# One-half feed-forward blocks beside the RWKV mixer: down projection in plain float32 products, and slots rounded to 64 bytes

## The chip, the cores and the metric

The kernel runs on one core of a Trainium2 chip. The metric is the device time of one execution in microseconds (us). Four compute engines matter here: TensorE (PE in the profile, with its weight loads as PEld), VectorE (DVE), ScalarE (ACT), and SyncE (SP), which issues all the loads.

## The reference, cut to what matters

Two layers work on 256 tokens of width 1024. Each layer is a feed-forward block, a token mixer with a memory attention, and a second feed-forward block, each followed by a layer norm. Layer 0 mixes with RWKV-7, a recurrence over tokens; layer 1 with stick-breaking attention.

```
swiglu(x, w_gate, w_up, w_down) = (silu(x @ w_gate) * (x @ w_up)) @ w_down     # d_ff = 2816

for i in range(2):
    x = layer_norm(ALPHA*x + 0.5*swiglu(x, ffn1[i]), ...)
    proj = x @ w_in[i]
    mix = rwkv7_mix(proj) if i == 0 else stick_breaking_mix(proj)
    x = layer_norm(ALPHA*x + concat(mix, memory_attention(proj)) @ w_out[i], ...)
    x = layer_norm(ALPHA*x + 0.5*swiglu(x, ffn2[i]), ...)
```

All inputs and the output are float32.

## The kernel before

**Tiles.** The 256 tokens are two halves of 128 (hf 0 and 1), the partitions of every tile. A feed-forward block is cut along d_ff into 11 blocks c of 256 columns (`FC`, `NFC`). One block for one half is 8 steps of a gate/up product (contraction over 1024, 512 columns wide: 256 gate and 256 up), the gating on ACT and DVE, a transposition of the 128x256 result by PE, and the down product: 2 steps of contraction times 2 column halves of 512.

**Split products.** A weight piece of 128x1024 is loaded into a `raw` buffer; ACT copies it to a rounded float32r tile `hi`, and DVE subtracts to get the rest, `lo` (`piece`, L636). The activations are split the same way (`split_T`, L675). `mm3` (L664) then makes one product of float32 operands as three float32r matmuls: hi by hi, hi by lo, lo by hi. There are 10 raw buffers and 9 each of hi and lo (`NRAW`, `NHI`, `NLO`). A raw buffer is free again when `lo` has been made; hi and lo are free when the last matmul has read them. A block needs six pieces: four of gate and up, two of down. The vectors of a layer norm sit in two raw buffers, too.

**Stages.** Half 1 runs behind half 0, so that one half's mixer, a long chain of small steps, has feed-forward blocks of the other half beside it. `LAGS` (L47) says how many blocks of a feed-forward are done for each half alone ("solo"); the rest are "shared": their pieces are loaded and split once and used for both halves (`spread`, L1415). For layer 0 the order is: blocks of FFN1 for half 0 (5 solo and 6 shared), norm of half 0, RWKV of half 0 with the 5 solo blocks of half 1 beside it (the first of them, `HEAD`, just ahead of it), norm of half 1, `w_out` and norm of half 0, RWKV of half 1 with solo blocks of FFN2 of half 0 beside it (`alternate`, L1403), `w_out` and norm of half 1, the last two solo blocks of half 0 (`HOLD`, L52), then the solo blocks of half 1 and the shared ones.

**Order.** The program is not written in the order in which it runs. `Plan` records every operation with a guessed duration; `order` (L346) is a list scheduler with priorities, which also hands out buffers, and `improve` (L542) repeats it with the latest start times as priorities, some noise, and a fixed seed. The numbers in `RW` (L50) say how far the blocks advance at each step of the mixer when the program is recorded, so they set the first priorities only. Any change of the recorded operations therefore gives another order everywhere behind it. Within an engine the order is then fixed, and all loads stand in one queue, SP's: a load whose buffer isn't free holds back those behind it. `copy` (L209) may go to ACT or DVE as the scheduler likes.

**Names.** The profile shows the buffers: `raw_*`, `hi_*`, `lo_*`; `xTh` and `xTl`, the split, transposed input of a stage; `h_*`, a block's gated result; `hT_*` and `pT_*` (one tag, `tb`, with two slots), its transposition; `ps_29` and `ps_30`, the gate/up banks; `ps_25` to `ps_28`, the down sums of half 0 (25, 26) and half 1 (27, 28); `ps_2` and `ps_3`, banks of transpositions and of the mixer; `S`, `T`, `Tt`, `Y`, `L`, `Lm`, `Sk`, `lb`, `vn`, `kn`, `bn`: the mixer's own. All recorded operations have the line of the issuing loop, L599.

**Slots.** All tiles of one tag share slots of the largest size asked for (`slot`, L165); the tag `tb` holds up to 4 x 129 floats, 2064 bytes a partition, so its second slot begins 2064 bytes after the first, rounded up to 32 by the allocator.

Of the kernel before, what the change touches and what calls it, by code (L numbers as in the profile page):

```python
# [13 lines left out]
F32 = mybir.dt.float32  # L14
F32R = mybir.dt.float32r
# [6 lines left out]
P = 128  # L22
D = 1024
# [19 lines left out]
NRAW = 10  # L43
NHI = 9
NLO = 9
HEAD = 1
LAGS = ((5, 9), (4, 8))  # L47
FIRST = 2
PRE = (0, 3)
RW = dict(p0=0, p1=2, p2=0, p3=0, p4=0, lb=0, sub=14, rb=0, kq=1, nat=0.5, dy=3, dt=2, c0=1.0, c1=1, c2=1.5, c3=2, t0=12, t1=10)  # L50
SB = dict(z0=3.0, z1=0, ln=2.0, e0=1.0, e1=1.5, o=6.0)
HOLD = (2, 4)  # L52
TAIL = (2, 2)
# [3 lines left out]
SHY = 1000.0  # L57
BOOST = 18.0075
BESIDE = (True, False)


BLK = 16
_LEVELS = [16, 32]

# [66 lines left out]
class Plan:  # L131
# [33 lines left out]
    def slot(self, pool, shape, dtype, tag, name, bufs):  # L165

        handle = bass.PSumTensorHandle if pool.name == "ps" else bass.SBTensorHandle
        tile = handle(name, list(shape), dtype)[:]
        key = pool.name, tag
        self.tag_of[name] = key  # L170
        self.pools[key] = pool
        self.slots[key] = max(bufs, self.slots.get(key, 0))
        self.size[key] = max(int(np.prod(shape[1:])), self.size.get(key, 0))
        return tile

    def region(self, ap):
# [426 lines left out]
def kernel(ctx, tc, const, x, mem, f1g, f1u, f1d, f2g, f2u, f2d, ln_g, ln_b, w_out, w_mem_kv,  # L603
                      rw_in, r_mu, r_w0, r_wup, r_a0, r_aup, r_gup, r_kk, r_ka, r_rk, r_lng, r_lnb, sb_in, out):
    nc = Plan(tc.nc)
# [4 lines left out]
    def nm(s):  # L610
        uid[0] += 1
        return f"{s}_{uid[0]}"

    def new(pool, shape, dtype, tag, name, bufs=1):

        return nc.slot(pool, shape, dtype, tag, nm(name), bufs)
# [19 lines left out]
    def piece(shape, *srcs):  # L636

        n = int(np.prod(shape))
        hi = new(wp, [P, D], F32R, "hi", "hi", NHI)[:, :n]
        lo = new(wp, [P, D], F32R, "lo", "lo", NLO)[:, :n]  # L640
        raw = new(wp, [P, D], F32, "raw", "raw", NRAW)[:, :n]
        v = lambda t: t.rearrange("p (a b) -> p a b", a=shape[0]) if len(shape) == 2 else t
        m = shape[-1] // len(srcs)
        made = [nc.sync.dma_start(v(raw)[..., i * m:(i + 1) * m], src) for i, src in enumerate(srcs)]
        for o in made:
            nc.in_turn("load", o)
        first = nc.scalar.activation(hi, raw, AF.Copy)
        nc.in_turn("hi", first)
        made.append(nc.vector.tensor_sub(lo, raw, hi.bitcast(F32)))
        nc.in_turn("lo", made[-1])  # L650
        nc.lead.update((o.i, first.i) for o in made + [first])
        return v(hi), v(lo)
# [11 lines left out]
    def mm3(o, sh, sl, wh, wl, start, stop):  # L664
        with nc.together():
            nc.tensor.matmul(o, sh, wh, start=start, stop=False)
            nc.tensor.matmul(o, sh, wl, start=False, stop=False)
            nc.tensor.matmul(o, sl, wh, start=False, stop=stop)
# [13 lines left out]
    def to_T(src, dst, j0, n):  # L682

        for g in range(0, n, 4):
            m = min(4, n - g)
            pt = ps("tp")
            with nc.together():
                for i in range(m):
                    nc.tensor.transpose(pt[:, i * P:(i + 1) * P], src[:, (g + i) * P:(g + i + 1) * P], ident)
            split_T(pt, dst, j0 + g, m)  # L690
# [44 lines left out]
    acc = [None] * NHALF  # L735
# [35 lines left out]
            turn_x(hf)  # L771


    def ffn_block(w, c, halves, beside):
        gv, uv, dv = (m.rearrange("(k p) c -> p k c", p=P) for m in w)
        fs = slice(c * FC, (c + 1) * FC)
        gu = [piece((2, 2 * FC), *(v[:, 2 * g:2 * g + 2, fs] for v in (gv, uv))) for g in range(4)]
        dn = [piece((D,), dv[:, 2 * c + q, :]) for q in range(2)]
        state = {}
        for hf in halves:  # L780
            if todo[hf] == 0:
                open_acc(hf)
                todo[hf] = NFC
            state[hf] = todo[hf] == NFC, todo[hf] == 1
            todo[hf] -= 1

        def down(hf, hh, hl):
            first, last = state[hf]
            for f, n in ((0, 0), (1, 0), (0, 1), (1, 1)) if last else ((0, 0), (0, 1), (1, 0), (1, 1)):
                sl = slice(n * 512, (n + 1) * 512)  # L790
                yield mm3(acc[hf][n], hh[:, f], hl[:, f], dn[f][0][:, sl], dn[f][1][:, sl], first and f == 0, last and f == 1)

        def gated(dst, g, u):

            if beside:
                nc.scalar.activation(dst, g, AF.Tanh, scale=0.5)
                nc.vector.scalar_tensor_tensor(dst, dst, 1.0, g, ALU.add, ALU.mult)
                nc.vector.scalar_tensor_tensor(dst, dst, 0.5, u, ALU.mult, ALU.mult)
            else:
                nc.scalar.activation(dst, g, AF.Silu)  # L800
                nc.vector.tensor_tensor(dst, dst, u, ALU.mult)


        o = {hf: ps("gu") for hf in halves}
        for k in range(KT):
            wh, wl = (t[:, k % 2] for t in gu[k // 2])
            for hf in halves:
                mm3(o[hf], xT[hf][0][:, k], xT[hf][1][:, k], wh, wl, k == 0, k == KT - 1)
            yield
        hs = {}  # L810
        for hf in halves:
            hs[hf] = new(tp_, [P, FC], F32, "ta", "h", 2)
            gated(hs[hf], o[hf][:, :FC], o[hf][:, FC:])

        def turn_h():
            res = []
            for hf in halves:
                hT = new(tp_, [P, 2, 2, P], F32R, "tb", "hT", 2)
                to_T(hs[hf], (hT[:, 0], hT[:, 1]), 0, 2)
                res.append(down(hf, hT[:, 0], hT[:, 1]))  # L820
            return res

        return turn_h
# [574 lines left out]
    def run(*gens):  # L1398
        for g in gens:
            for _ in g:  # L1400
                pass

    def alternate(main, fill, steps):  # L1403

        due = 0.0
        n = next(main, None)
        while n is not None:
            due += steps.get(n, 0)
            while due >= 1.0:
                next(fill, None)  # L1410
                due -= 1.0
            n = next(main, None)
        run(fill)
# [4 lines left out]
        seq += [((i + 0.49) / len(shared), c, range(NHALF)) for i, c in enumerate(shared)]  # L1418
        return [(c, h) for _, c, h in sorted(seq, key=lambda t: t[0])]

    def blocks(w, seq, beside=False):
        waiting = []
        for c, halves in seq:
            hidden = yield from ffn_block(w, c, halves, beside)
            yield from chain(*waiting)
            waiting = hidden()
        yield from chain(*waiting)

    def solo(hf, cs):
        return [(c, [hf]) for c in cs]  # L1430
# [5 lines left out]
    for i in range(DEPTH):  # L1436
        mixer, steps = ((rwkv, RW), (stick, SB))[i % 2]
        last = i == DEPTH - 1
        lag1, lag2 = LAGS[i]
        w = f1g[i], f1u[i], f1d[i]  # L1440
        if i == 0:
            seq = spread((0, range(lag1)), range(lag1, NFC))
            run(blocks(w, seq[:2]))
            nc.in_turn("load", nc.sync.dma_start(cst[:, P:], const[:, P:]))
            run(blocks(w, seq[2:4]))
            rwkv_constants()
            gb = ln_g[i, 0], ln_b[i, 0]
            run(blocks(w, seq[4:]))
        else:
            run(blocks(w, solo(0, range(FIRST))))  # L1450
            gb = ln_g[i, 0], ln_b[i, 0]
            run(blocks(w, spread((0, range(FIRST, lag1)), range(lag1, NFC))))
        norm(0, 2.0 * ALPHA, 4.0 * LN_EPS, gb)
        mixed = []
        run(blocks(w, solo(1, range(HEAD)), BESIDE[0]))
        if i == 0:
            run(memory_kv())
        alternate(chain_steps(mixer(0, mixed)), blocks(w, solo(1, range(HEAD, lag1)), True), steps)
        norm(1, 2.0 * ALPHA, 4.0 * LN_EPS, gb)
        gb = ln_g[i, 1], ln_b[i, 1]  # L1460
        w = f2g[i], f2u[i], f2d[i]
        second = chain_steps(mixer(1, mixed))
        for _ in range(PRE[i]):
            next(second)
        run(chain_steps(mixed_out(0, mixed[0], w_out[i])))
        norm(0, ALPHA, LN_EPS, gb)
        alternate(second, blocks(w, solo(0, range(lag2 - HOLD[i])), True), steps)
        run(chain_steps(mixed_out(1, mixed[1], w_out[i])), blocks(w, solo(0, range(lag2 - HOLD[i], lag2)), BESIDE[1]))
        norm(1, ALPHA, LN_EPS, gb)
        gb = ln_g[i, 2], ln_b[i, 2]  # L1470
        run(blocks(w, spread((1, range(TAIL[i], lag2)), range(lag2, NFC))))
        norm(0, 2.0 * ALPHA, 4.0 * LN_EPS, gb, last)
        run(blocks(w, solo(1, range(TAIL[i]))))
        norm(1, 2.0 * ALPHA, 4.0 * LN_EPS, gb, last)
# [25 lines left out]
```

## Time and profile before

| | us |
|---|---|
| median of 3 runs (1101.57 to 1103.51) | 1103.34 |
| span of the profiled execution, first to last instruction | 1099.8 |
| PE busy | 1062.8 (97%) |
| DVE busy | 928.8 (84%) |
| ACT busy | 751.6 (68%) |

The profiled execution's own time is given by its span; the median of the runs lies 3.5 us above that (launch and end). The page cuts the span into 40 slices; a stage has other limits than the whole, so the windows of a stage are read for what bounds it. A matmul's shown duration (some 390 ns for 512 columns) is longer than the distance between two starts (some 230 ns), since they are pipelined: PE's busy share hides short gaps, and distances between starts are what a product costs. The same holds on DVE, less strongly.

### The profile page before, as it was taken

Reading aid. Unit: us, or ns where it says so; the run is one execution under the profiler, and the core shown is the slowest. Engines: PE = TensorE matmul, PEld = TensorE weight load, DVE = VectorE, ACT = ScalarE, POOL = GpSimd, SP = SyncE. Lnnn points to the kernel's source line nnn. Section 1 sums busy time; section 2 is a strip of 40 time slices with the busy share of each in tenths; the row PEclk is TensorE's granted clock in tenths of the full one; section 3 lists DMA queues with packets and bytes.
Section 4 is the critical chain, followed back from the end, with each engine's and each line's share of the span. In section 5 each row is a group of like instructions: output and inputs, shape, how many; then the busy total and the mean of one; then the engine's idle time right before and its main releaser. Section 6 shows DMA issues by size and latency. Waiting matters only on the chain.

```text
span 1099.8 us, 17711 instructions
## 1 busy us (share of the span) xinstructions
PE 1062.8 (97%) x6265; PEld 861.4 (78%) x6265; DVE 928.8 (84%) x1312; ACT 751.6 (68%) x1021; POOL 2.7 (0%) x14
## 2 busy tenths in 40 slices
PE   7999999998799999999999999999999999999996
PEld 6878887876678787778888888888877877888885
DVE  6567677999999999998889965649899989987777
ACT  7466566987369786676668654547898898866652
POOL 0000000000000000000000000000000000000000
PEclk9999999999989999999999999999999999999998
DMA  9499758866679587799989976657987987998781
GB/s 344 149 363 378 262 203 291 295 216 204 190 226 336 179 288 251 256 297 369 323 271 362 352 244 212 206 195 258 392 292 269 349 284 266 376 379 292 264 289 59
DMA packets 212250, 303.30 MB, mean 276 GB/s; under 512 B 13844, under 2 KB 159424, under 8 KB 212162
## 3 DMA queue, kind: packets, MB, share of 16 engines
q1 hardware_dynamic: 212162, 302.18, 80.5%
q8 instruction: 49, 0.80, 0.3%
q14 instruction: 39, 0.32, 0.1%
HBM read 301.08 MB, written 1.05 MB: 275 GB/s over the span
## 4 chain that ended last, share of the span: by engine, by line
PE 79%; DVE 13%; DMA 3%; issue 2%; ACT 2%; SPq 0%; DVEq 0%; ACTq 0%
PE ps_30r L599 25%; PE ps_29r L599 24%; PE ps_26r L599 6%; PE ps_25r L599 6%; PE ps_28r L599 6%; PE ps_27r L599 6%; PE ps_2r L599 3%; PE ps_3r L599 3%; DVE x L599 1%; DMA raw_45r<-in_ffn_w_up_dram 1%; DVE lo_44r L599 1%; DVE lb_498r L599 1%; DMA raw_21r<-in_ffn_w_up_dram 1%; DVE lo_20r L599 1%; DVE lo_17r L599 1%
## 5 line engine op out<-in xcount | busy, mean ns | idle before, releaser
L599 ACT ACTIVATE h_32r<-ps_30r 128x256 f32<-128x256 f32 (+1 forms) x35 | 15.1, 431 | 23.1 <-PE ps_30r L599 23.1
L599 ACT ACTIVATE h_31r<-ps_29r 128x256 f32<-128x256 f32 (+1 forms) x34 | 14.5, 426 | 18.5 <-PE ps_29r L599 18.5
L599 PE MATMUL ps_30r<-hi_22r,xTh 128*128 128x512 f32 x64 | 26.3, 410 | 0.0
L599 PE MATMUL ps_30r<-hi_22r,xTl 128*128 128x512 f32 x64 | 25.0, 391 | 0.0
L599 PE MATMUL ps_30r<-lo_23r,xTh 128*128 128x512 f32 x64 | 25.0, 391 | 0.0
L599 PE MATMUL ps_30r<-hi_10r,xTh 128*128 128x512 f32 (+1 forms) x58 | 23.0, 397 | 0.0
L599 PE MATMUL ps_29r<-hi_16r,xTh 128*128 128x512 f32 x56 | 22.4, 401 | 0.0
L599 PE MATMUL ps_29r<-hi_40r,xTh 128*128 128x512 f32 (+1 forms) x56 | 22.4, 401 | 0.0
L599 PE MATMUL ps_30r<-hi_10r,xTl 128*128 128x512 f32 (+1 forms) x58 | 22.3, 385 | 0.0
L599 PE MATMUL ps_30r<-lo_11r,xTh 128*128 128x512 f32 (+1 forms) x58 | 22.2, 383 | 0.0
L599 PE MATMUL ps_29r<-hi_16r,xTl 128*128 128x512 f32 x56 | 21.9, 391 | 0.0
L599 PE MATMUL ps_29r<-lo_17r,xTh 128*128 128x512 f32 x56 | 21.9, 391 | 0.0
L599 PE MATMUL ps_29r<-hi_40r,xTl 128*128 128x512 f32 (+1 forms) x56 | 21.5, 384 | 0.0
L599 PE MATMUL ps_29r<-lo_41r,xTh 128*128 128x512 f32 (+1 forms) x56 | 21.5, 383 | 0.0
L599 PE MATMUL ps_30r<-hi_13r,xTh 128*128 128x512 f32 x52 | 21.4, 412 | 0.0
L599 PE MATMUL ps_30r<-hi_7r,xTh 128*128 128x512 f32 x52 | 21.2, 408 | 0.0
L599 PE MATMUL ps_30r<-lo_14r,xTh 128*128 128x512 f32 x52 | 20.5, 394 | 0.4 <-DVE lo_14r L599 0.4
L599 PE MATMUL ps_2r<-cst,x 128*128 128x128 f32 x48 | 8.9, 316 | 12.2 <-DVE x L599 6.7
L599 PE MATMUL ps_29r<-lo_44r,xTh 128*128 128x512 f32 x50 | 19.7, 395 | 0.9 <-DVE lo_44r L599 0.8
L599 PE MATMUL ps_30r<-lo_17r,xTh 128*128 128x512 f32 x50 | 19.7, 393 | 0.8 <-DVE lo_17r L599 0.8
L599 PE MATMUL ps_30r<-hi_7r,xTl 128*128 128x512 f32 x52 | 20.4, 392 | 0.0
L599 PE MATMUL ps_30r<-hi_13r,xTl 128*128 128x512 f32 x52 | 20.4, 392 | 0.0
(1923 smaller groups left out, 4044.8 us busy)
## 6 DMA issues: line engine op xcount, KB each, us to landing
raw_45r<-in_ffn_w_down_dram SPq DMA_DIRECT2D x17, 512.0 KB, 4.1
raw_24r<-in_ffn_w_down_dram SPq DMA_DIRECT2D x16, 512.0 KB, 4.6
raw_15r<-in_ffn_w_gate_dram SPq DMA_DIRECT2D x30, 256.0 KB, 4.6
raw_15r<-in_ffn_w_up_dram SPq DMA_DIRECT2D x30, 256.0 KB, 5.6
raw_21r<-in_ffn_w_down_dram SPq DMA_DIRECT2D x15, 512.0 KB, 6.3
raw_39r<-in_ffn_w_gate_dram SPq DMA_DIRECT2D x30, 256.0 KB, 4.8
raw_39r<-in_ffn_w_up_dram SPq DMA_DIRECT2D x30, 256.0 KB, 4.9
raw_42r<-in_ffn_w_down_dram SPq DMA_DIRECT2D x15, 512.0 KB, 5.1
```

What stands on the lines that cost most here:

```text
L599: fn(*[at(x) for x in a], **{n: at(x) for n, x in k.items()})
```

## The change

In blocks that a list `WHOLE` names, the two down pieces are loaded into raw buffers and used as they are: no `hi`, no `lo`. The transposed result is copied once, unsplit, and the down product is one plain float32 matmul in place of three float32r ones. The list is asked for only in the solo blocks beside the RWKV mixer and right ahead of and behind it. It names all five of FFN1 for half 1, and of FFN2 for half 0 all but block 3. A second edit moves one block of layer 0's FFN2 from solo to shared (`LAGS`, 9 to 8), so that seven solo blocks of half 0 are whole: twelve in all, 48 products. Four step numbers in `RW` change, and slot sizes are rounded up to 16 floats.

```diff
-LAGS = ((5, 9), (4, 8))
+LAGS = ((5, 8), (4, 8))
-RW = dict(p0=0, p1=2, ..., rb=0, ..., dy=3, ..., t0=12, t1=10)
+RW = dict(p0=0, p1=0, ..., rb=0.5, ..., dy=4, ..., t0=0, t1=10)
+WHOLE = (((0, 1, 2, 3, 4, 5, 6, 8, 9, 10), (0, 1, 2, 4, 5, 6, 7, 8, 9)), ((), ()))
+LINE = 16
...
-        self.size[key] = max(int(np.prod(shape[1:])), self.size.get(key, 0))
+        self.size[key] = max(-(-int(np.prod(shape[1:])) // LINE) * LINE, self.size.get(key, 0))
...
-        dn = [piece((D,), dv[:, 2 * c + q, :]) for q in range(2)]
+        if whole:
+            dn = [new(wp, [P, D], F32, "raw", "raw", NRAW) for _ in range(2)]
+            for q, t in enumerate(dn):
+                nc.in_turn("load", nc.sync.dma_start(t, dv[:, 2 * c + q, :]))
+        else:
+            dn = [piece((D,), dv[:, 2 * c + q, :]) for q in range(2)]
...
+                if whole:
+                    yield nc.tensor.matmul(acc[hf][n], h[0][:, f], dn[f][:, sl], start=start, stop=stop)
+                else:
+                    yield mm3(acc[hf][n], h[0][:, f], h[1][:, f], dn[f][0][:, sl], dn[f][1][:, sl], start, stop)
...
+                if whole:
+                    hT = new(tp_, [P, 2, P], F32, "tb", "hT", 2)
+                    nc.copy(hT, turned(hs[hf], 0, 2))
+                    res.append(down(hf, hT))
...
-        run(blocks(w, solo(1, range(HEAD)), BESIDE[0]))
+        run(blocks(w, solo(1, range(HEAD)), BESIDE[0], WHOLE[i][0]))
-        alternate(second, blocks(w, solo(0, range(lag2 - HOLD[i])), True), steps)
+        alternate(second, blocks(w, solo(0, range(lag2 - HOLD[i])), True, WHOLE[i][1]), steps)
```

On PE, in the first mixer just behind the scores of the memory attention (`memKT`), a block's down product stood like this before:

```order
L599 MATMUL ps_26r<-memKT,mq_357r 128x256
L599 MATMUL ps_3r<-cst,h_32r 128x128 x2
L599 MATMUL ps_27r<-hi_43r,hT_502r 128x512
L599 MATMUL ps_27r<-lo_44r,hT_502r 128x512
L599 MATMUL ps_27r<-hi_43r,hT_502r 128x512
L599 MATMUL ps_28r<-hi_43r,hT_502r 128x512
```

At the same place the changed program has (`pT_352r` is the slot in which the transposed result lies):

```order
L601 MATMUL ps_26r<-memKT,mq_353r 128x256
L601 MATMUL ps_3r<-cst,h_32r 128x128 x2
L601 MATMUL ps_30r<-hi_19r,xTh 128x512
L601 MATMUL ps_30r<-lo_20r,xTh 128x512
L601 MATMUL ps_30r<-hi_19r,xTl 128x512
L601 MATMUL ps_27r<-raw_39r,pT_352r 128x512
L601 MATMUL ps_28r<-raw_39r,pT_352r 128x512
L601 MATMUL ps_27r<-raw_45r,pT_352r 128x512
L601 MATMUL ps_28r<-raw_45r,pT_352r 128x512
```

Twelve matmuls became four, and three gate/up matmuls stand ahead of them. On SP, at the end of the first mixer, the loads of the norm's vectors and of `w_out` stood in these buffers before:

```order
L599 DMA raw_9r<-in_ln_g_dram 128x1024
L599 DMA raw_12r<-in_ln_b_dram 128x1024
L599 DMA raw_39r<-in_w_out_dram 128x2x512
L599 DMA raw_42r<-in_w_out_dram 128x2x512
L599 DMA raw_18r<-in_w_out_dram 128x2x512
L599 DMA raw_24r<-in_w_out_dram 128x2x512
L599 DMA raw_15r<-in_w_out_dram 128x2x512
L599 DMA raw_21r<-in_w_out_dram 128x2x512
```

In the changed program they stand in these, with the whole down pieces of the last blocks in `raw_15r` and `raw_18r` and others:

```order
L601 DMA raw_21r<-in_ln_g_dram 128x1024
L601 DMA raw_42r<-in_ln_b_dram 128x1024
L601 DMA raw_45r<-in_w_out_dram 128x2x512
L601 DMA raw_9r<-in_w_out_dram 128x2x512
L601 DMA raw_12r<-in_w_out_dram 128x2x512
L601 DMA lb_475r<-in_rwkv_lnx_b_dram 128x768
L601 DMA raw_24r<-in_w_out_dram 128x2x512
L601 DMA raw_45r<-in_w_out_dram 128x2x512
L601 DMA raw_9r<-in_w_out_dram 128x2x512
```

`raw_45r` and `raw_9r` are loaded again by the fourth load behind the last one into them (of those into raw buffers); before, it was the eighth at the soonest, everywhere in the program. On DVE the same twelve blocks lose 24 `lo` subtractions and 12 of the split results, and the block that is now shared loses six more `lo` (540 to 510 in the program).

More of the change, by code (lines that the diff above doesn't have):

```diff
@@ L46 @@
 HEAD = 1
-LAGS = ((5, 9), (4, 8))
+LAGS = ((5, 8), (4, 8))
 FIRST = 2
 PRE = (0, 3)
-RW = dict(p0=0, p1=2, p2=0, p3=0, p4=0, lb=0, sub=14, rb=0, kq=1, nat=0.5, dy=3, dt=2, c0=1.0, c1=1, c2=1.5, c3=2, t0=12, t1=10)
+RW = dict(p0=0, p1=0, p2=0, p3=0, p4=0, lb=0, sub=14, rb=0.5, kq=1, nat=0.5, dy=4, dt=2, c0=1.0, c1=1, c2=1.5, c3=2, t0=0, t1=10)
 SB = dict(z0=3.0, z1=0, ln=2.0, e0=1.0, e1=1.5, o=6.0)
@@ L771, in norm, with ffn_block @@
             turn_x(hf)
-    def ffn_block(w, c, halves, beside):
+    def ffn_block(w, c, halves, beside, whole):
         gv, uv, dv = (m.rearrange("(k p) c -> p k c", p=P) for m in w)
@@ L785, in ffn_block, with down @@
             todo[hf] -= 1
-        def down(hf, hh, hl):
+        def down(hf, *h):
             first, last = state[hf]
@@ L790, in down @@
                 sl = slice(n * 512, (n + 1) * 512)
-                yield mm3(acc[hf][n], hh[:, f], hl[:, f], dn[f][0][:, sl], dn[f][1][:, sl], first and f == 0, last and f == 1)
+                start, stop = first and f == 0, last and f == 1
+                if whole:
+                    yield nc.tensor.matmul(acc[hf][n], h[0][:, f], dn[f][:, sl], start=start, stop=stop)
+                else:
+                    yield mm3(acc[hf][n], h[0][:, f], h[1][:, f], dn[f][0][:, sl], dn[f][1][:, sl], start, stop)
         def gated(dst, g, u):
@@ L817, in turn_h @@
             for hf in halves:
-                hT = new(tp_, [P, 2, 2, P], F32R, "tb", "hT", 2)
-                to_T(hs[hf], (hT[:, 0], hT[:, 1]), 0, 2)
-                res.append(down(hf, hT[:, 0], hT[:, 1]))
+                if whole:
+                    hT = new(tp_, [P, 2, P], F32, "tb", "hT", 2)
+                    nc.copy(hT, turned(hs[hf], 0, 2))
+                    res.append(down(hf, hT))
+                else:
+                    hT = new(tp_, [P, 2, 2, P], F32R, "tb", "hT", 2)
+                    to_T(hs[hf], (hT[:, 0], hT[:, 1]), 0, 2)
+                    res.append(down(hf, hT[:, 0], hT[:, 1]))
             return res
@@ L1419, in spread, with blocks @@
         return [(c, h) for _, c, h in sorted(seq, key=lambda t: t[0])]
-    def blocks(w, seq, beside=False):
+    def blocks(w, seq, beside=False, whole=()):
         waiting = []
         for c, halves in seq:
-            hidden = yield from ffn_block(w, c, halves, beside)
+            hidden = yield from ffn_block(w, c, halves, beside, c in whole)
             yield from chain(*waiting)
@@ L1454 @@
         mixed = []
-        run(blocks(w, solo(1, range(HEAD)), BESIDE[0]))
+        run(blocks(w, solo(1, range(HEAD)), BESIDE[0], WHOLE[i][0]))
         if i == 0:
             run(memory_kv())
-        alternate(chain_steps(mixer(0, mixed)), blocks(w, solo(1, range(HEAD, lag1)), True), steps)
+        alternate(chain_steps(mixer(0, mixed)), blocks(w, solo(1, range(HEAD, lag1)), True, WHOLE[i][0]), steps)
         norm(1, 2.0 * ALPHA, 4.0 * LN_EPS, gb)
@@ L1466 @@
         norm(0, ALPHA, LN_EPS, gb)
-        alternate(second, blocks(w, solo(0, range(lag2 - HOLD[i])), True), steps)
-        run(chain_steps(mixed_out(1, mixed[1], w_out[i])), blocks(w, solo(0, range(lag2 - HOLD[i], lag2)), BESIDE[1]))
+        alternate(second, blocks(w, solo(0, range(lag2 - HOLD[i])), True, WHOLE[i][1]), steps)
+        run(chain_steps(mixed_out(1, mixed[1], w_out[i])), blocks(w, solo(0, range(lag2 - HOLD[i], lag2)), BESIDE[1], WHOLE[i][1]))
         norm(1, ALPHA, LN_EPS, gb)
```

## The prediction

> **What bounds the kernel now.** I read the page first: its busy times, and its slices.
>
> ```profile
> span 1099.8 us, 17711 instructions
> PE 1062.8 (97%) x6265; PEld 861.4 (78%) x6265; DVE 928.8 (84%) x1312; ACT 751.6 (68%) x1021; POOL 2.7 (0%) x14
> PE   7999999998799999999999999999999999999996
> DVE  6567677999999999998889965649899989987777
> PEclk9999999999989999999999999999999999999998
> ```
>
> PE is close to full everywhere, DVE only in slices 8 to 18 and in the second layer's mixers. Slices 10 to 12 (27.5 us each), where PE has gaps and loses clock, lie at the end of the first RWKV mixer. Next I cut windows where DVE closes the statistics of the layer norms (152, 294, 322, 478, 571, 606). Columns: busy us of PE, PEld, DVE, ACT, POOL with counts, granted clock, DMA share, GB/s.
>
> ```profile
> 152.00:228.00 76.00, 75.58 (x425) 61.92 (x424) 69.03 (x116) 60.29 (x87) 0.21 (x1) 1.00 0.82 278
> 228.00:294.00 66.00, 61.49 (x832) 49.26 (x832) 64.36 (x115) 44.25 (x80) 0.20 (x1) 0.97 0.61 204
> 294.00:322.00 28.00, 21.49 (x153) 17.92 (x152) 27.47 (x59) 13.66 (x17) 0.43 (x2) 0.82 0.64 197
> 322.00:400.00 78.00, 76.18 (x573) 60.73 (x572) 77.78 (x142) 64.55 (x105) 0.21 (x1) 1.00 0.80 267
> 400.00:478.00 78.00, 76.50 (x792) 62.08 (x791) 76.23 (x119) 54.79 (x77) 0.00 (x0) 1.00 0.80 263
> 478.00:571.00 93.00, 91.80 (x417) 75.14 (x416) 79.62 (x96) 62.81 (x76) 0.00 (x0) 1.00 0.94 324
> 571.00:606.00 35.00, 35.00 (x163) 28.78 (x162) 34.51 (x49) 27.28 (x33) 0.00 (x0) 1.00 0.98 341
> 606.00:748.00 142.00, 142.00 (x644) 116.66 (x643) 92.36 (x116) 73.21 (x95) 0.00 (x0) 1.00 0.72 237
> ```
>
> From 322 to 478, the second RWKV mixer, DVE works 154.0 of 156 us; from 228 to 294, 64.4 of 66. From 478 on PE is the bound: 142 of 142 us in the plain feed-forward. The chain of waits says the same of the first mixer: in 228 to 303 it runs mostly through DVE, and much of it is `lo` subtractions (start, length, what):
>
> ```profile
> 235.13 1.23 DVE lo_17r L599
> 236.36 1.13 DVE lo_23r L599
> 237.49 1.14 DVE lo_11r L599
> 238.63 1.14 DVE lo_14r L599
> ```
>
> So beside the mixers DVE ends last, outside them PE. The change takes work from DVE beside the mixers and gives work to PE: the question is whether a stretch beside a mixer shortens by more than PE's new work adds elsewhere.
>
> **DVE's relief.** The timeline of DVE gives the price of what goes, as distances between starts (columns: start, duration, instruction).
>
> ```profile
> 263.23 0.40 DVE L599 TENSOR_TENSOR hT_545r<-ps_2r,hT_545r 128x256 fp32r<-128x256 f32 x1
> 263.56 0.40 DVE L599 SCALAR_TENSOR_TENSOR h_32r<-h_32r,ps_30r 128x256 f32<-128x256 f32 x1
> 275.48 1.22 DVE L599 TENSOR_TENSOR lo_44r<-raw_42r,hi_43r 128x1024 fp32r<-128x1024 f32 x1
> 276.61 1.22 DVE L599 TENSOR_TENSOR lo_20r<-raw_18r,hi_19r 128x1024 fp32r<-128x1024 f32 x1
> 277.75 1.22 DVE L599 TENSOR_TENSOR lo_11r<-raw_24r,hi_10r 128x1024 fp32r<-128x1024 f32 x1
> 278.88 0.55 DVE L599 TENSOR_TENSOR Tt_358r<-Tt_358r,ps_3r 128x384 f32<-128x384 f32 x1
> ```
>
> A `lo` costs 1.13 us of DVE's time, a split result (`hT`) 0.33. In passing one sees the recurrence's own step (`Tt`) queued behind three `lo`. Counting `lo` in DVE's order between the norms' statistics: 152 to 294 has 53 instead of 61; 294 to 322 8 for 9; 322 to 478 58 for 75 (eleven by whole pieces, six because one block of FFN2 becomes shared). With the split results that is 8 x 1.13 + 4 x 0.33 = 10.4 us, 1.1 us, and 17 x 1.13 + 9 x 0.33 = 22.2 us (the 9 are seven whole blocks and two gating steps of the moved block). ACT loses as many `hi` copies, which costs and gains nothing: it is busy 44 to 65 us in windows of 66 to 78.
>
> **PE's price.** A plain float32 product of 512 columns by 128 rows does not stand in this trace. The nearest row is one of 384 columns, which the profile shows as two matmuls:
>
> ```profile
> 201.56 0.39 PE L599 MATMUL ps_29r<-hi_16r,xTh 128*128 128x512 f32 x1
> 201.79 0.40 PE L599 MATMUL ps_29r<-lo_17r,xTh 128*128 128x512 f32 x1
> 202.02 0.39 PE L599 MATMUL ps_29r<-hi_16r,xTl 128*128 128x512 f32 x1
> 202.25 0.81 PE L599 MATMUL ps_25r<-gup_108r,zl_340r 128*128 128x384 f32 x2
> 202.90 0.81 PE L599 MATMUL ps_26r<-gup_108r,zl_340r 128*128 128x384 f32 x2
> 203.54 0.60 PE L599 MATMUL ps_3r<-cst,h_32r 128*128 128x128 f32 x4
> ```
>
> The split product is three starts 0.23 apart, 0.69 us. The plain one takes 0.645 for 384 columns, so by columns 0.86 for 512: 0.17 more, 48 times, 8.2 us. Bounds: no longer than the 384-column row itself (0.645: 2.2 us gained), or as long by columns as that row's shown duration of 0.81 (1.08: 18.7 us). I take 0.86, since the two rows at 202.25 and 202.90 follow each other without a gap. The Trainium skill (FP8 and Floating Point Precision, TensorE Precision Notes) counts four passes for a true float32 product. By it the product would cost 4 x 0.23 = 0.92, all 48 of them 11.0 us, and my sum below would end 2.8 us higher; the 384-column row speaks for a little less (0.645, where four passes at 384/512 of 0.23 make 0.69), and I keep the row.
>
> By PE's order, between the transpositions behind each norm, float32r products and whole ones change so: first mixer 360 to 300 and 20 whole (-60 x 0.23 + 20 x 0.86 = +3.4 us); up to half 0's norm 105 to 90 (-3.4); second mixer 447 to 354 and 24 (-0.8); the stretch of 478 to 571 414 to 465 and 4 (+15.2: the shared block is done for both halves there, and the last whole one); all behind it 27 fewer (-6.2: the solo block that half 1 no longer has). Sum +8.2, as it must be.
>
> A new wait: the whole product waits for its load and for one copy of the transposed result, where it waited for two `lo` and a split result. Everything behind it on PE waits with it, first the next gate/up product; as down pieces are loaded a block ahead, I cost this at nothing beyond the rival on raw buffers below.
>
> **Slots.** Products with the two slots of `hT` differ (min/median/max ns):
>
> ```profile
> L599 PE MATMUL ps_26r<-hi_10r,hT_876r x8: 389/390/397, 410.3 to 713.3; 128*128 128x512 f32 x8
> L599 PE MATMUL ps_26r<-hi_22r,hT_903r x6: 392/397/501, 401.7 to 669.5; 128*128 128x512 f32 x6
> ```
>
> `hT_903r` is the second slot, which starts 32 bytes off a multiple of 64; each product with it is 6 ns longer. Half of the 88 half-blocks' 12 down products use it, some 460 after the change: up to 2.8 us, which rounding may take away; at least 0. I take 2. The other tiles are small and on no path.
>
> **Sum.** First mixer: DVE could give 10.4 us, PE needs 3.4 more of it. PE has room there (4.9 us idle from 152 to 294, and clock 0.97), but the recurrence also waits on PE and ACT, so I take two thirds of DVE's relief: -7 (ends -10.4 and +3.4). To half 0's norm: -1.5 (ends -3.4 and 0), since the norm's small steps on DVE stay. Second mixer: DVE's 22.2 us can't all come out, since PE is busy 152.7 of 156 and its work falls by 0.8 only; but its shown busy time hides gaps that a slow chain leaves. I take -9 (ends -22.2 and -0.8). Then +15.2, on a PE that is full: all of it on the path. Behind it -6.2, where PE is full too. Slots -2. Total -10.5: a span of 1089.3 us, and with the 3.5 us by which the median of the runs lies above this span, 1092.8 us.
>
> **The rivals.**
>
> *The chain keeps its length (slower).* If the recurrence is held by its own steps on PE, DVE and ACT rather than by the `lo` between them, the three stretches up to 478 keep their length, and what is left is +15.2 - 6.2 - 2 = +7: 1110.3 us. For it: PE and ACT, not DVE, are on the chain in parts of the first mixer, and clock 0.82 from 294 to 322 shows a chain too thin to keep PE up. Against it: DVE idles 1.6 us from 228 to 294 and 2.0 from 322 to 478. It decides if the three stretches together give less than 7 us.
>
> *DVE sets every microsecond.* All of its relief comes out: -10.4 - 1.1 - 22.2 + 7 = -26.7, 1076.6 us. Against it: PE would then do its work of the second mixer in 134 us instead of 156.
>
> *Raw buffers run short.* A whole piece keeps its raw buffer until its down product, behind the next block's gate/up. In the changed order of SP a raw buffer is loaded again by the fourth load after the last one, at the end of the first mixer and around the last whole blocks; eight to ten before.
>
> ```profile
> raw_45r<-in_ffn_w_down_dram SPq DMA_DIRECT2D x17, 512.0 KB, 4.1
> raw_21r<-in_ffn_w_down_dram SPq DMA_DIRECT2D x15, 512.0 KB, 6.3
> L599 ACT ACTIVATE hi_10r<-raw_21r 128x1024 fp32r<-128x1024 f32 x11 | 11.7, 1065 | 5.9 <-PE ps_27r L599 3.1 <-DMA raw_48r<-in_ffn_w_gate_dram 1.7 <-PE ps_28r L599 0.3
> ```
>
> A buffer's round is 4.1 to 6.3 us to land, 1.1 for `hi`, 1.1 for `lo`: some 8 us, with four buffers a piece each 2.1 us. Beside the mixer a piece is wanted each 2.3 us or so (142 us for 61 `lo`), which still fits. In the stretch from 478 it doesn't: a solo block is 36 x 0.23 = 8.3 us for six pieces, 1.4 us each, and over some nine pieces at depth four PE would wait 9 x 0.7 = 6 us, unless the pieces that are made already cover it: 1099 us.
>
> *It does nothing where it counts.* The scheduler gives back in another place what it gains here: 1103.
>
> **How the numbers follow.** My sum, 0.48 (1084 to 1098); raw buffers 0.18; chain 0.15; all of DVE 0.14; nothing 0.05. A measurement of this kernel tells some 0.2% (2.2 us) from no change. Faster: 0.48 + 0.14 + 0.11 of the raw buffers; same: 0.05, 0.05 of the raw buffers and 0.02 of the chain; slower: the rest, 0.15. The range goes from 1080 to 1107: it leaves out half of the rival at 1077 and somewhat over half of the one at 1110, about 0.16.
>
> **What would show it.** In the new profile: 48 products of `ps_25` to `ps_28` from `raw`, as 96 records some 0.43 us apart; DVE below 95% from 322 to the second norm of half 1; that stretch near 147 us and the first mixer's near 135; 15 us more from there to the next norm; products with the second `hT` slot at 390 ns. The sum is wrong if DVE has new idle time that ends with a landing (raw buffers), or if DVE gets idle time that ends with PE or ACT and the stretches stay (chain); the price of a product is wrong if its records lie closer than 0.4 or further than 0.46 us apart.

## The result, and the profile after

The change is faster by 0.8%: 1094.03 us median of 4 runs (1093.15 to 1096.41) against 1102.78 (1101.57 to 1103.51); ratio 0.9924, 95% interval 0.9912 to 0.9936. The forecast was 1092.8. A second measurement of the same kernel, beside the experiments on slots, gave 1094.16 and a ratio of 0.9922 (0.9910 to 0.9935); its profile has a span of 1092.0 us and is called the second profile below.

The page of the profile after, the same lines as of before, and under them the shares of the chain that ended last:

```profile
span 1094.4 us, 17466 instructions
PE 1067.0 (97%) x6217; PEld 852.9 (78%) x6217; DVE 895.0 (82%) x1269; ACT 719.9 (66%) x991; POOL 2.7 (0%) x14
...
PE   7999999999799999999999999999989999999996
...
DVE  6577676999999998787779965659799989987777
...
PEclk9999999999899999999999999999999999999999
...
PE 90%; DVE 6%; DMA 2%; issue 1%; ACT 1%; SPq 0%; DVEq 0%; ACTq 0%
```

The chain's shares before were:

```profile
PE 79%; DVE 13%; DMA 3%; issue 2%; ACT 2%; SPq 0%; DVEq 0%; ACTq 0%
```

DVE has 34 us less work and PE 4 us more busy time. At the end of the first mixer PE has one slice with gaps where it had two. The chain that ended last is 90% PE and 6% DVE, where it was 79% and 13%. Windows cut at the same events as before (DVE closes a norm's statistics; columns as in the prediction):

```profile
152.00:228.00 76.00, 75.96 (x426) 61.70 (x425) 65.65 (x118) 57.33 (x84) 0.20 (x1) 1.00 0.80 266
228.00:290.00 62.00, 61.68 (x822) 45.04 (x823) 58.28 (x100) 37.91 (x73) 0.39 (x2) 1.00 0.70 241
290.00:317.00 27.00, 21.22 (x143) 17.96 (x138) 25.77 (x54) 13.16 (x17) 0.24 (x2) 0.81 0.66 199
317.00:390.00 73.00, 73.00 (x552) 57.55 (x551) 71.60 (x140) 57.92 (x97) 0.20 (x1) 1.00 0.76 259
390.00:464.00 74.00, 74.00 (x762) 56.40 (x761) 63.86 (x100) 43.62 (x64) 0.00 (x0) 1.00 0.80 261
464.00:572.00 108.00, 108.00 (x476) 85.99 (x475) 83.60 (x100) 66.48 (x84) 0.00 (x0) 1.00 0.88 299
```

In the second mixer DVE works 135.5 of 147 us, where it had 154.0 of 156, and PE's shown gaps are gone there. The chain says it more sharply: before, it runs through DVE for 70 of the 156 us from 322 to 478 (31 of them `lo`), after the change, from 317 to 464, for none: all of it is PE. The bound has moved from DVE to PE. To the tenth, by the starts of the same events:

| stretch | before | after | difference | forecast |
|---|---|---|---|---|
| first RWKV mixer | 141.0 | 137.3 | -3.7 | -7 |
| to half 0's norm | 28.1 | 27.6 | -0.5 | -1.5 |
| second RWKV mixer | 156.4 | 146.5 | -9.9 | -9 |
| to the next norm (one more shared block) | 93.3 | 107.9 | +14.6 | +15.2 |
| all behind it | 528.6 | 522.8 | -5.8 | -6.2 |

The plain product's price, in the timeline of PE (start, shown length, what; the three lines with `raw` are a product each, shown as two records, between a float32r matmul and a transposition):

```profile
466.12 0.39 PE L601 MATMUL ps_30r<-hi_13r,xTl 128*128 128x512 f32 x1
466.34 1.02 PE L601 MATMUL ps_25r<-raw_18r,hT_304r 128*128 128x512 f32 x2
467.20 1.02 PE L601 MATMUL ps_26r<-raw_18r,hT_304r 128*128 128x512 f32 x2
468.06 1.02 PE L601 MATMUL ps_26r<-raw_42r,hT_304r 128*128 128x512 f32 x2
468.92 0.38 PE L601 MATMUL ps_3r<-cst,h_31r 128*128 128x128 f32 x2
```

It is 0.86 us from start to start, as the 384-column row said. Four passes, the count of the Trainium skill (FP8 and Floating Point Precision, TensorE Precision Notes), would be 0.92 us if each took the 0.23 of this trace's float32r matmuls, which is an estimate. For the time, the measured 0.86 decides. It doesn't refute the count: four passes of 0.215 us each would give it, too, and no run here parts the two.

### The profile page after: what moved, and what is told of

Read it like the earlier page. It is cut to its first block, busy times and chain, and to the rows that moved or that the text cites. A ratio compares the mean times of both kernels' runs of the same rounds, so it can differ in the third digit from the quotient of the medians.

```text
span 1094.4 us, 17466 instructions
## 1 busy us (share of the span) xinstructions
PE 1067.0 (97%) x6217; PEld 852.9 (78%) x6217; DVE 895.0 (82%) x1269; ACT 719.9 (66%) x991; POOL 2.7 (0%) x14
## 4 chain that ended last, share of the span: by engine, by line
PE 90%; DVE 6%; DMA 2%; issue 1%; ACT 1%; SPq 0%; DVEq 0%; ACTq 0%
PE ps_30r L601 27%; PE ps_29r L601 27%; PE ps_28r L601 8%; PE ps_27r L601 8%; PE ps_25r L601 7%; PE ps_26r L601 7%; PE ps_2r L601 3%; PE ps_3r L601 3%; DVE x L601 1%; DMA raw_45r<-in_sb_w_in_dram 1%; DMA raw_21r<-in_ffn_w_up_dram 1%; DMA raw_9r<-in_ffn_w_up_dram 1%; DVE lb_475r L601 0%; DVE lo_8r L601 0%; DVE S_110r L601 0%
## 5 line engine op out<-in xcount | busy, mean ns | idle before, releaser
L601 ACT ACTIVATE h_31r<-ps_30r 128x256 f32<-128x256 f32 (+1 forms) x53 | 22.8, 430 | 33.6 <-PE ps_30r L601 33.6
L601 ACT ACTIVATE h_32r<-ps_29r 128x256 f32<-128x256 f32 (+1 forms) x53 | 22.0, 414 | 30.0 <-PE ps_29r L601 29.6
L601 PE MATMUL ps_29r<-hi_37r,xTh 128*128 128x512 f32 x58 | 24.2, 417 | 0.0
L601 PE MATMUL ps_29r<-hi_37r,xTl 128*128 128x512 f32 x58 | 22.7, 392 | 0.0
L601 PE MATMUL ps_29r<-lo_38r,xTh 128*128 128x512 f32 x58 | 22.6, 390 | 0.0
L601 PE MATMUL ps_30r<-hi_16r,xTh 128*128 128x512 f32 x54 | 22.6, 418 | 0.0
L601 PE MATMUL ps_29r<-hi_22r,xTh 128*128 128x512 f32 (+1 forms) x54 | 21.9, 406 | 0.0
L601 PE MATMUL ps_30r<-hi_10r,xTh 128*128 128x512 f32 x54 | 21.9, 405 | 0.0
L601 PE MATMUL ps_30r<-hi_40r,xTh 128*128 128x512 f32 x52 | 21.8, 420 | 0.0
L601 PE MATMUL ps_30r<-hi_16r,xTl 128*128 128x512 f32 x54 | 21.2, 392 | 0.0
```

Of the source, the lines that this page charges most:

```text
L601: fn(*[at(x) for x in a], **{n: at(x) for n, x in k.items()})
```

## The experiments

My theory: the whole pieces' relief of DVE beside the RWKV mixers pays for PE's longer products. Its rivals: the moved block, the new order, the loads.

**Which part of the change it is.** Whole pieces off, the rest of the change on:

```diff
-WHOLE = (((0, 1, 2, 3, 4, 5, 6, 8, 9, 10), (0, 1, 2, 4, 5, 6, 7, 8, 9)), ((), ()))
+WHOLE = (((), ()), ((), ()))
```

> The changed kernel with the list of whole blocks empty: the moved block, the step numbers and the slots stay. Theory (the whole pieces' relief of VectorE beside the RWKV mixers is the gain): moving a block takes 8.3 us of PE work each from the second mixer and from half 1's solo blocks and gives 16.6 us to the stretch behind the mixer, so it is about even; 1098 to 1104 us, VectorE at 97% or more from the first mixer to the end of the second. Rival (the moved block is the gain): 1092 to 1096 us.

Measured: 1107.45 us, ratio 1.0038 (1.0023 to 1.0053): slower than before. The rival is refuted, my range was 3.5 us too low, and "about even" was wrong: the move costs. The windows:

```profile
228.00:295.00 67.00, 60.54 (x805) 47.32 (x805) 66.09 (x110) 44.98 (x79) 0.40 (x2) 1.00 0.71 233
...
322.00:398.00 76.00, 71.77 (x552) 57.42 (x551) 74.89 (x142) 61.49 (x100) 0.21 (x1) 1.00 0.79 263
398.00:475.00 77.00, 74.09 (x779) 58.90 (x778) 73.97 (x113) 51.90 (x73) 0.00 (x0) 1.00 0.73 239
475.00:580.00 105.00, 104.80 (x475) 85.69 (x475) 85.03 (x103) 67.00 (x83) 0.00 (x0) 1.00 0.90 303
```

DVE is again at 96 to 99% beside the mixers, and PE shows 6.5 us idle in the first of these windows and 7.1 in the next two. The moved block shortened the second mixer's stretch by 3.8 us only (152.6), though it took 8.3 us of PE work out, and lengthened the next one by 11.7 (105.0).

The other way round, whole pieces with the old split of solo and shared:

```diff
-LAGS = ((5, 8), (4, 8))
+LAGS = ((5, 9), (4, 8))
```

> The changed kernel with nine solo blocks of FFN2 in layer 0 as before (eight of them whole, 13 whole blocks in all). Theory: most of the gain stays, 1093 to 1098 us. Rival (the moved block is the gain): 1100 us or more.

Measured: 1098.7 us, ratio 0.9956 (0.9942 to 0.9971): the theory's side, a little over its range. So the four kernels are: before 1103.1 (measured beside these two; 1102.2 and 1102.4 beside later experiments), the move without whole pieces 1107.5, whole pieces without the move 1098.7, both 1094.0 to 1094.2. Whole pieces give 4.4 us without the move and 13.3 with it; the move costs 4.4 without them and gives 4.5 with them. The middle two also have the changed step numbers and slots, and whole pieces without the move are 13 blocks, not 12. No run has the step numbers alone; the 13.3 us are free of them, since both kernels have them.

**Is it DVE's work?** The same products on PE, but `hi` and `lo` are made as before and not read (this kernel does work that nothing uses):

```diff
...
+                hi = new(wp, [P, D], F32R, "hi", "hi", NHI)
+                lo = new(wp, [P, D], F32R, "lo", "lo", NLO)
+                first = nc.scalar.activation(hi, t, AF.Copy)
...
+                rest = nc.vector.tensor_sub(lo, t, hi.bitcast(F32))
...
```

> The changed kernel, but hi and lo of the whole pieces are made as well and not read: 24 more subtractions of 1.13 us on VectorE and 24 more copies on ScalarE, all else as in the change, PE's plain float32 products too. Theory (VectorE's queue sets the stretches beside the mixers): both stretches go back to what they took before and PE's price stays, 1104 to 1112 us. Rival (the fewer, longer products of PE or the new order are the gain, and VectorE's work is covered): 1092 to 1098 us.

Measured: 1108.19 us, ratio 1.0041 (1.0027 to 1.0055), 14 us over the change, in the middle of the theory's range. Its windows:

```profile
228.00:293.00 65.00, 61.32 (x776) 43.75 (x776) 63.00 (x106) 44.72 (x79) 0.20 (x1) 1.00 0.65 221
...
322.00:398.00 76.00, 74.12 (x545) 57.71 (x544) 73.73 (x139) 60.52 (x100) 0.21 (x1) 0.98 0.71 239
398.00:474.00 76.00, 74.15 (x760) 55.92 (x759) 72.97 (x110) 50.99 (x73) 0.00 (x0) 1.00 0.76 253
```

DVE is back at 96 to 97%, PE's gaps are back, and the mixers' stretches take 141.1 and 152.7 us: 137.3 and 146.5 in the change, 142.7 and 152.6 without whole pieces. So 10.0 of the 14 us lie beside the mixers; the rest is spread over later stretches and isn't explained here. In the window of the second mixer the chain again runs through DVE, for 28 us, 12 of them `lo`. This kernel also holds more `hi` and `lo` buffers than the change and keeps ACT's copies, and its order differs. ACT's busy time grows as DVE's does (37.9 to 44.7 us in the window from 228, DVE 58.3 to 63.0), but ACT is busy for only 67 to 80% of these windows. What this run shows is that making the split pieces costs the time; that DVE's share in it is the larger is read from the chain and the windows, and the buffers aren't tested apart.

**Is it the order?** Another seed of the search (`SEED` 144 to 145), the same operations:

> The changed kernel with another seed of the order's search (145 for 144): the same operations in another order. It measures how far orders alone differ. Theory: within 4 us of the change's 1094 us, 1090 to 1098. Rival (the gain is a lucky order): 1099 us or more.

Measured: 1096.5 us, ratio 0.9935 (0.9921 to 0.9950). The other order costs 2.3 us and keeps 6.6 us of the gain, so the gain isn't a lucky order of the changed kernel. This is one more order, and the kernel before was measured with one only. Differences of 2 to 3 us between the kernels above, whose orders differ, shouldn't be explained one by one, and the 4.4 and 4.5 of the move are only about twice that.

**Each mixer alone.**

```diff
+WHOLE = (((0, 1, 2, 3, 4), ()), ((), ()))
```

> The changed kernel with whole blocks beside the first RWKV mixer alone (five blocks, 20 products). The kernel without any took 1107.5 us, the change 1094.2. Theory (each mixer's stretch gives its own part: 5.4 us in the first and 6.1 in the second, between these two kernels): 1100 to 1104 us, the first mixer's stretch near 137 us, the second's near 152. Rival (both relieve one shared queue of loads, so that one part alone gives little or nearly all): 1106 or more, or 1097 or less.

Measured: 1102.27 us, ratio 0.9998 (0.9988 to 1.0008). Stretches: 137.2 and 152.0 us, as expected.

```diff
+WHOLE = (((), (0, 1, 2, 4, 5, 6, 7)), ((), ()))
```

> The changed kernel with whole blocks in FFN2 beside the second mixer alone (seven blocks, 28 products). Theory: 1099 to 1104 us, the first mixer's stretch near 142 us, the second's near 147. Rival: as for the first mixer alone.

Measured: 1101.64 us, ratio 0.9994 (0.9985 to 1.0004). Stretches: 142.5 us as expected, and 149.5, which is 2.5 over what was expected. From the 1107.5 without any, the first gives 5.2 us and the second 5.8, together 11.0 of the 13.3 that both give: each stretch pays for itself, and the two nearly add, within what another order moves.

**Raw buffers.** `NRAW` 10 to 12, `NHI` and `NLO` 9 to 8:

> The changed kernel with 12 raw buffers and 8 each of hi and lo in place of 10, 9 and 9 (the same memory). Theory (whole pieces keep raw buffers and loads come late in the first mixer, where VectorE now waits 9 us for ScalarE, which waits for a landing): 2 to 4 us faster than the change. Rival (the loads are covered): within 2 us of the change, or slower, as hi and lo are short.

Measured: 1098.72 us, ratio 0.9965 (0.9953 to 0.9978): 4.6 us slower than the change. The first mixer's stretch is 136.0 us, 1.3 shorter, the second's 149.3, 2.8 longer. The theory is refuted: raw buffers at the price of `hi` and `lo` don't pay. That it got slower may lie in the fewer `hi` and `lo` or in the other order, which this run doesn't part, so it doesn't say either what more raw buffers alone would give.

**Slots.** Without the rounding, every engine's order the same:

```diff
-LINE = 16
+LINE = 1
```

> The changed kernel without the rounding of slots; every engine's order is the same. Prediction on record: up to 2.8 us slower than the change, 2 taken. By the trace of the change (second slot still 235 ns): no difference, within 1 us.

Measured: 1093.41 us, ratio 0.9920 (0.9907 to 0.9934), the change 1094.16: no difference, where the prediction took 2 us. Then other roundings for the tag `tb` alone:

```diff
-        self.size[key] = max(-(-int(np.prod(shape[1:])) // LINE) * LINE, ...)
+        self.size[key] = max(-(-int(np.prod(shape[1:])) // (64 if tag == "tb" else LINE)) * (64 if tag == "tb" else LINE), ...)
```

> The changed kernel with the slots of the tag tb rounded to 256 bytes, all others to 64; every engine's order is the same. In the trace of the change the second hT slot, now at a multiple of 64, is still slower (235 ns from start to start against 227). Theory (the weight read wants a larger alignment, of 128 or 256 bytes): 227 ns in both slots, 1 to 3 us less. Rival (something else than the address): 235 ns and no change of time.

Measured: 1091.87 us (1090.60 to 1092.41), ratio 0.9901 (0.9887 to 0.9914): 2.3 us faster than the change, and the fastest kernel of this study. The two intervals overlap by a little, so the rows below have to bear this out. With 34 floats in place of 64, the second slot at 128 bytes past a multiple of 256:

> The changed kernel with the second slot of the tag tb at an odd multiple of 128 bytes; every engine's order is the same. It tells which alignment the product wants: if 128 bytes suffices, 227 ns from start to start in both slots and the 2.3 us that 256 bytes gave; if 256 bytes is needed, 230 ns or more in the second and no gain.

Measured: 1093.82 us, ratio 0.9921 (0.9905 to 0.9936): no gain. The rows of one group of products with the second slot follow (shown lengths, min/median/max ns). By the sizes, the second slot begins 2080, 2112, 2176 or 2304 bytes after the first, which lies at a multiple of 256 in the built programs. First the change, where the second slot lies 64 bytes past such a multiple, with one group of the first slot below it:

```profile
L601 PE MATMUL ps_28r<-hi_7r,hT_1053r x8: 393/394/399, 492.4 to 750.2; 128*128 128x512 f32 x8
```

```profile
L601 PE MATMUL ps_28r<-hi_37r,hT_1077r x6: 389/390/390, 511.0 to 741.8; 128*128 128x512 f32 x6
```

The same group of the second slot at 32 bytes past such a multiple (no rounding), at 128 bytes, and at the multiple:

```profile
L601 PE MATMUL ps_28r<-hi_7r,hT_1053r x8: 392/395/397, 492.0 to 749.8; 128*128 128x512 f32 x8
```

```profile
L601 PE MATMUL ps_28r<-hi_7r,hT_1053r x8: 390/394/404, 490.5 to 748.5; 128*128 128x512 f32 x8
```

```profile
L601 PE MATMUL ps_28r<-hi_7r,hT_1053r x8: 389/389/398, 489.4 to 745.8; 128*128 128x512 f32 x8
```

From start to start, as the median of all float32r products that read the slot, the second one takes 232 ns at 32 bytes, 235 at 64, 232 at 128 and 227 at 256; the first slot takes 227 to 228 everywhere.

**Beside the other mixer too.** The 256-byte slots, and the solo blocks beside the stick-breaking mixer whole as well:

```diff
-WHOLE = ((...), ((), ()))
+WHOLE = ((...), (tuple(range(11)), tuple(range(11))))
```

> The changed kernel with the 256-byte slots (1091.9 us) and with the solo blocks beside the stick-breaking mixer whole as well: twelve blocks, 48 products, 8.2 us more for PE, 24 lo of 1.13 us less for VectorE. Theory (relief pays only where VectorE is full and PE has room; beside this mixer VectorE is at 92 to 97% and PE has some 7 us without work): no gain or slower, 1090 to 1098 us. Rival (whole pieces pay beside any mixer): 1088 us or less.

Measured: 1103.54 us, ratio 1.0008 (0.9998 to 1.0017): 11.7 us slower than with the same slots and no whole pieces there, more than PE's 8.2. The rival is refuted, and the theory's range was too low by 5.5. Windows with whole pieces in layer 1 (first feed-forward; half 0's mixer; half 1's mixer):

```profile
602.00:749.00 147.00, 147.00 (x669) 121.27 (x668) 98.18 (x121) 76.93 (x99) 0.00 (x0) 1.00 0.76 243
749.00:822.00 73.00, 71.88 (x330) 51.88 (x328) 56.15 (x72) 56.62 (x81) 0.00 (x0) 1.00 0.81 281
857.00:946.00 89.00, 89.00 (x448) 64.59 (x447) 68.62 (x94) 68.94 (x100) 0.00 (x0) 1.00 0.83 284
```

and without, cut at the same events:

```profile
601.00:737.00 136.00, 136.00 (x620) 112.17 (x619) 87.51 (x109) 69.32 (x89) 0.00 (x0) 1.00 0.72 232
737.00:814.00 77.00, 75.35 (x379) 60.72 (x378) 70.23 (x90) 67.34 (x93) 0.00 (x0) 1.00 0.94 325
850.00:937.00 87.00, 87.00 (x470) 68.64 (x468) 80.15 (x106) 79.64 (x114) 0.00 (x0) 1.00 0.88 301
```

DVE's share in the two mixers' windows falls from 91 and 92% to 77 and 77%, but the three windows together take 309 us instead of 300: PE was full or nearly full in them already (75.4 of 77 us and 87 of 87 in the mixers' windows), and the order moved PE's work to the first of them (669 matmuls instead of 620), where it is full, too. Where the 3.5 us beyond PE's price of 8.2 come from is open.

## Why the prediction was right, point by point

**The bound.** Right from 228 us to the end of the first mixer and in the whole second mixer: there DVE was full and much on the chain. Giving the split pieces back, without touching PE's products, cost 14 us, 10.0 of them beside the mixers. From 152 to 228 it was wrong, as follows.

**The first mixer** was the term that was mis-sized: -7 was taken, -3.7 measured (141.0 to 137.3, and 137.5 in the second profile). The step that failed is "DVE could give 10.4 us", which counted `lo` from 152 to 294 as one stretch. The prediction's own rows show two: from 152 to 228 DVE worked 69.0 of 76 us and PE 75.6, and the chain there was PE for 71 of the 76 us. What DVE lost there (3.4 us, three of the eight `lo`) bought nothing, and after the change PE has 76.0 of 76. In both traces most of the mixer's own steps around 228 lie within 2 us of each other, so the cut parts the same work. Only from 228 on was DVE full. There it lost 6.1 us of work (64.4 to 58.3), the window shortened by 4.0, and PE's shown idle time fell from 4.5 to 0.3. The chain there still runs through DVE for 24 of the 62 us, where it was 32 of 66, so DVE and PE bound this part together, and not all of its relief came out. DVE's waits in the first of the two windows (who waited, us, times, longest) show the relief turned into idle time. Before they were

```profile
DVE lo_11r L599 <- ACT hi_10r L599: 3.5, 1, 3.5
DVE lo_14r L599 <- ACT hi_13r L599: 1.7, 1, 1.7
DVE lo_17r L599 <- ACT hi_16r L599: 0.9, 2, 0.6
```

and after, with 10.4 us of idle time in the same 76 us where there were 7.0:

```profile
DVE lo_14r L601 <- ACT hi_13r L601: 3.1, 1, 3.1
DVE lo_11r L601 <- ACT hi_10r L601: 3.1, 2, 2.1
DVE lo_41r L601 <- ACT hi_40r L601: 2.1, 1, 2.1
```

**To half 0's norm**: -1.5 taken, -0.5 measured, and -1.7 in the second profile (26.4): within what two profiles of one kernel differ.

**The second mixer**: -9 taken, -9.9 measured. Here DVE was full in both windows, and the limit is now PE, as reasoned: it has no shown gap left, and the chain is PE alone. How much PE's shown busy time hid was a guess, and it was a good one.

**The price on PE**: 0.86 us a product taken and measured. So +15.2 came out as +14.6, and -6.2 as -5.8, in stretches where PE is full and work counts fully.

**Slots**: -2 taken, 0 measured. The step that failed is "which rounding may take away": that a slot at a multiple of 64 bytes would be as fast as the first. The slower second slot was seen rightly (6 ns a product), but at a multiple of 64 it is as slow (235 ns from start to start), so that 64 bytes changes nothing; 256 gives the 2.3 us.

**The sum**: -10.5 was forecast on the span; the two spans here differ by 5.4 (1099.8 and 1094.4), the second profile of the change has 1092.0, 7.8 under it, and the medians differ by 8.8. The terms' errors are +3.3 in the first mixer, +1.0 behind it, -0.9, -0.6, +0.4 and +2.0 for the slots: 5.2 together, which are the 5.1 between -10.5 and -5.4. The two spans lie at opposite ends: every measured time is 1.7 to 2.8 us above its span, so 1099.8 can only belong to the fastest of the three runs before, while the profiled execution of the change was its slowest (1096.41, others 1093.15 to 1094.05). So not all of the "3.5 us" that were added are launch and end, as was said: some 2 are, and the rest is that one execution. That the median came within 1.2 us of the forecast is in part luck: two terms were 5.3 us too favourable together, and against them stand small errors the other way and the differences between executions.

**The rivals.** That the chain keeps its length: the three stretches gave 14.1 us, over the 7 where it begins. That DVE sets every microsecond: in the second mixer PE took over. Raw buffers: in the stretch behind the second mixer, where this rival lets PE wait 6 us, PE has 108.00 of 108 us. DVE waits more for ACT in the first mixer, but where the chain is PE's. That it does nothing where it counts: 1103 was its time, and 1094 is clear of it.

## What to carry to other kernels

Trading a helper engine's work for a longer product paid here only in stretches where the helper was full and TensorE showed gaps; cut the windows finely enough that "full" holds in every one before counting the relief, and look for the price in the stretches where TensorE is full. Two edits that each look even may need each other: moving work out of a stretch cost 4.4 us here while the helper bounded it, and gained 4.5 once it didn't, though one other order alone moved 2.3. A slower slot of a rotating buffer is seen in the trace by comparing the same group of matmuls between slots.

## What the runs showed of the hardware

A float32r product of 512 columns whose 128x128 stationary operand begins at a multiple of 256 bytes in its partition started every 227 ns here; at 32, 64 or 128 bytes past such a multiple, every 232 to 235 ns. Why is open. Over some 430 products, most of them where TensorE is full, 256 bytes gave 2.3 us (1094.16 to 1091.87) with every engine's order unchanged; 8 ns each would be 3.4. A plain float32 product of the same size is two records 0.43 us apart, 0.86 us, against 0.69 for three float32r ones.
